# Weights of a two-block transformer: transfers of 8 KB rows, splits of 1024 columns, a gelu of one operation

## The chip, the cores and the metric

One core of a Trainium2 chip runs the whole program in one launch; the batch is one sequence of 256 tokens. The metric is device time in microseconds of one execution, the median of three runs. An engine is written as the profile writes it: PE is TensorE (matmuls; PEld its weight loads), DVE is VectorE, ACT is ScalarE, POOL is GpSimd, SP is the engine whose queue issues nearly all transfers.

## The reference

Two blocks, all in float32, D = 1024, 256 tokens.

- First block, one layer. An rmsnorm and one wide projection `w_in` give a gated linear recurrence (conv of 4 taps, sigmoid gates, a scan), a differential attention of 4 heads and a forgetting attention of 8 heads. Three gated branches are merged and projected. Then `u = causal_dwconv(h @ ffn_up)` with 2816 gate and 2816 value columns, and `x + (gelu(u_gate) * u_val) @ ffn_down`, where gelu is the tanh form.
- Second block, two layers. A mixer (a dilated attention of 12 small heads and a window attention of 16 heads, gates, two branches, an output projection), then 16 experts of width 1024 with expert-choice routing: `softmax(h @ w_router)`, each expert takes its 32 best tokens, and
  `a = xe @ w_gate; u = xe @ w_up; ye = (silu(a) * u) @ w_down` is added back, weighted by the router.

The weights are read once: 141 MB (of 2^20 bytes) of dense weights and 192 MB of expert weights in each of the two layers.

## The kernel before

**Layout.** Activations lie with features on the 128 partitions and the 256 tokens along the free axis; x is `[128, 8, 256]`. Dense weights are packed on the host into loads of 1 MB, `[128, 2048]`: 16 blocks of 128x128.

**Dense work.** `load` (L115) brings one such MB in two transfers of 512 KB (128 rows of 4 KB) into two tiles of a ring of six (`R1 = 6`, `RW = 1024` columns). For float32 accuracy each weight is used as a rounded high part and a low part. `split_w` (L123) makes them for half a load (1024 columns) in two steps of 512 columns: ScalarE copies the high part into `wh` (L129), and VectorE and GpSimd in turn subtract it from the weight, for the low part `wl` (L132):

```python
nc.scalar.copy(wh, s)
turn[0] += 1
eng = nc.gpsimd if turn[0] % 2 == 0 else nc.vector
eng.tensor_tensor(wl, s, wh.bitcast(F32), op=ALU.subtract)
```

The pool of splits has eight `wh` and eight `wl` of 2 KB in a partition, so four halves of a load. The activations are split too (`h[0]` is Ha, `h[1]` is Hb), and `mm3` (L138) issues three matmuls for a block: high by high, high by low, low by high (L139 to L141). A load is therefore 48 matmuls of 256 columns.

**First block.** Stages in order: q, k, v of the two attentions with the attentions between them, the recurrence and its gates, the branch products, the output projection, 22 tiles of the up-projection, and the down-projection. A tile of the up-projection (L627) is one load, `over_rms` (L222) from PSUM, a conv of three taps for the gate and the value part (one ScalarE operation at L252 and two VectorE operations at L256 each), `gelu2` (L243: a square and a tanh on ScalarE, two VectorE operations at L246 and L248), the product with the value part (L639) and `split_act` (L166, L167). Its high parts go to Ah, its low parts to Ala (16 tiles) and Alb (6 tiles, the last ones).

**Mixers.** 23 loads of `w_in2`, 5 of `w_br2` and 4 of `w_out2`, with the window attention and the dilated attention between them. The window attention leaves one of its two softmax scalings to GpSimd (L845).

**Experts.** For each of four groups of four experts, gate, up and down are streamed through. `grouped` (L1208) multiplies the tokens of four experts, 32 partitions of PSUM each, by their weights, k after k; a matmul (L1219) has 32 stationary columns and 512 moving ones. Class `Experts` (L1017) decides where each transfer lands. Its list `todo` has (matrix, expert, rows, columns); `load` (L1039) cuts an item into halves of 4 KB in a partition, or gives it a whole place of 8 KB (two row blocks of 4 KB rows). The cycle of places is: 3 halves in the tiles Qb, 15 in pool a (4 of them, `NA0`, exist from the start of the mixer, 11 from the end of its attentions), then the wholes Ha, Hb and two of pool b, then the six tiles of the ring, four halves cut into pieces of 512 columns (2 KB rows) in the pool of splits, and, the first time only, five halves in W and XB. A place is filled again when its last matmul has read it. The last matrix of a layer comes in column pieces (`ENDS` = 512, 256, 256 columns), so that its transfers have rows of 2 KB and then 1 KB.

**Early transfers.** Part of a layer's experts is brought during the mixer. `prefetch` and `pace` issue these loads after chosen dense loads: 7 items after the window attention, then one `pace` after each load of the gates and branches, up to 13 items; two more (Ha, Hb) at the sixth branch tile, and two into pool b after it. A paced load first writes one column of its place from GpSimd, which reads the newest `wl`: the transfer waits for that split.

**Order.** The order within each engine's queue is written down ahead of the run by a list scheduler with its own cost model, from the program's order and the readiness of the operands. Every queue, SP's too, works in order; an instruction that waits holds what stands behind it.

Of the kernel before, what the change touches and what calls it, by code (L numbers as in the profile page):

```python
# [26 lines left out]

def _places(widths):
# [22 lines left out]
R1, RW, NA0, NA, R2B, NSPLIT, SW = 6, 1024, 4, 15, 2, 8, 512  # L51
# [3 lines left out]
PACE = 1  # L55
# [3 lines left out]
def tile_net(ctx: ExitStack, tc: tile.TileContext, a, out):  # L59
# [6 lines left out]
    ring = ctx.enter_context(tc.tile_pool(name="ring", bufs=R1, side="right"))  # L66
# [4 lines left out]
    first = [ring.tile([P, RW], F32, name="w", tag="w") for _ in range(0, CH, RW)]  # L71
    p1 = None

    def start(pool):
# [38 lines left out]
    turn = [0, None]  # L113

    def load(src):  # L115
        ws = []
        for c in range(0, CH, RW):
            w = ring.tile([P, RW], F32, name="w", tag="w")
            nc.sync.dma_start(w, src[:, c : c + RW])
            ws.append(w)  # L120
        return ws

    def split_w(sp, w, hf):  # L123
        his, los = [], []
        for c in range(hf * 1024, hf * 1024 + 1024, SW):
# [7 lines left out]
            turn[1] = wl  # L133
            his.append(wh)
            los.append(wl)
        return his, los
# [148 lines left out]
    def first_block():  # L285
        with ExitStack() as es:
# [31 lines left out]
            dk, dv = [qp.tile([P, 4, T], F32, name=nm, tag="Qb", bufs=3) for nm in ("dk", "dv")]  # L318
# [301 lines left out]
            with tc.tile_pool(name="b1f", bufs=2) as tp:  # L620
# [3 lines left out]
                for n in (4, 2):  # L624
                    Alb = qp.tile([P, n, T], F32R, name="Alb", tag="Qb", bufs=3)
                    Al += [Alb[:, k] for k in range(n)]
                for j in range(DFF_T):  # L627
# [10 lines left out]
                    gelu2(gg, u[:, 0, :])  # L638
# [470 lines left out]
    def experts(l, last, xl, bp, xg, lg, rt):  # L1109
        nonlocal x  # L1110
        with ExitStack() as es:
# [387 lines left out]
```

## Time and profile before

| | |
|---|---|
| median of 3 runs | 1959.91 us (1959.46 to 1960.38) |
| profiled execution | 1959.11 us, span 1957.1 us |
| busy, share of the span | PE 1665.0 us (85%), DVE 848.3 (43%), ACT 676.0 (35%), POOL 431.1 (22%) |
| mean granted TensorE clock | 0.946 of full speed |
| moved | 562.67 MB in 184744 packets, mean 288 GB/s |

The span is the time from the first to the last instruction; the 2.0 us between it and the execution's own time lie around the program. The busy shares are means over stages with different limits: dense stages (0 to about 785 us and 1240 to 1490) and expert stages (the rest), so they are read by stage. A matmul's busy time overlaps that of its neighbours; its pitch is read from counts in a window. MB and GB/s of the profile count 10^6 and 10^9 bytes.

### The profile page before, as it was taken

How to read it: one execution, taken by the hardware profiler on the slowest of the kernel's cores; microseconds unless marked ns; L12 is line 12 of the kernel's file. 1: busy time of each engine (PE TensorE's matmuls, PEld its weight loads, DVE VectorE, ACT ScalarE, POOL GpSimd, SP SyncE). 2: the span in 40 equal slices, each digit the busy share in tenths (PEclk: the TensorE clock that was granted, in tenths of full speed). 3: DMA queues.
4: the chain of work that ended last, by engine and by line, in shares of the span. 5: the costliest groups of instructions: out<-in, count | busy, mean ns of one | idle time of the engine just before them, and what ended most of it. 6: DMA issues, size and time to landing. Idle time of an engine off the chain costs nothing.

```text
span 1957.1 us, 29983 instructions
## 1 busy us (share of the span) xinstructions
PE 1665.0 (85%) x11434; PEld 1142.9 (58%) x11434; DVE 848.3 (43%) x1525; ACT 676.0 (35%) x1436; POOL 431.1 (22%) x368
## 2 busy tenths in 40 slices
PE   8899999998999998777767776999998587867775
PEld 8799999987998898222211211798995121212112
DVE  8578787998488556100000001686582100000001
ACT  5467656666666644000000000576552000000001
POOL 4333354444454253000000000443350000000000
PEclk9899999999999999888998998999999798989988
DMA  6454465444563379899999999854588999999998
GB/s 238 143 184 149 162 200 171 162 156 166 184 234 113 108 286 345 335 408 405 406 406 407 406 409 377 301 182 129 213 293 302 409 406 407 407 407 406 407 403 268
DMA packets 184744, 562.67 MB, mean 288 GB/s; under 512 B 17932, under 2 KB 39320, under 8 KB 184600
## 3 DMA queue, kind: packets, MB, share of 16 engines
q1 hardware_dynamic: 184440, 560.23, 77.1%
q8 instruction: 90, 1.47, 0.3%
q10 hardware_dynamic: 160, 0.52, 0.1%
q14 instruction: 54, 0.44, 0.1%
HBM read 558.84 MB, written 1.85 MB: 286 GB/s over the span
## 4 chain that ended last, share of the span: by engine, by line
PE 54%; DMA 38%; DVE 5%; issue 2%; ACT 1%; SPq 0%; ACTq 0%; DVEq 0%
DMA we<-in_w_expert_up_dram 16%; PE ps_d L139 12%; PE ps_d L141 12%; PE ps_d L140 12%; DMA we<-in_w_expert_down_dram 11%; DMA we<-in_w_expert_gate_dram 10%; PE ps_e L1219 3%; PE ps_g L1219 2%; PE ps_u L1219 2%; PE ps_t L266 1%; PE ps_v L854 1%; DVE wl L132 1%; PE ps_t L1235 1%; DVE u L256 1%; PE ps_s L382 1%
## 5 line engine op out<-in xcount | busy, mean ns | idle before, releaser
L132 POOL TENSOR_TENSOR wl<-w,wh 128x512 fp32r<-128x512 f32 x282 | 396.2, 1410 | 969.4 <-DMA w<-in_w_in_dram 479.2
L141 PE MATMUL ps_d<-Ha,wl 128*128 128x256 f32 x1408 | 405.7, 288 | 6.4 <-DVE wl L132 6.2
L139 PE MATMUL ps_d<-Ha,wh 128*128 128x256 f32 x1408 | 405.0, 288 | 7.0 <-ACT Ha L186 7.0
L140 PE MATMUL ps_d<-Hb,wh 128*128 128x256 f32 x1408 | 403.3, 286 | 2.0 <-DVE Hb L187 1.9
L129 ACT CAST wh<-w 128x512 fp32r<-128x512 f32 x564 | 334.9, 615 | 152.1 <-PE ps_d L140 111.9
L1219 PE MATMUL ps_u<-we,W 128*32 128x512 f32 x984 | 226.3, 731 | 121.2 <-DMA we<-in_w_expert_up_dram 121.2
L132 DVE TENSOR_TENSOR wl<-w,wh 128x512 fp32r<-128x512 f32 x282 | 239.2, 852 | 97.8 <-ACT wh L129 87.2
L141 PEld LDWEIGHTS ps_d<-Ha,wl 128*128 128x128 f32 x1408 | 271.7, 193 | 12.7 <-DVE wl L132 9.1
L139 PEld LDWEIGHTS ps_d<-Ha,wh 128*128 128x128 f32 x1408 | 271.9, 193 | 11.9 <-ACT Ha L186 7.0
L140 PEld LDWEIGHTS ps_d<-Hb,wh 128*128 128x128 f32 x1408 | 271.7, 193 | 5.0 <-DVE Hb L187 2.7
L1219 PE MATMUL ps_e<-we,W 128*32 128x512 f32 (+1 forms) x1152 | 198.2, 599 | 49.9 <-DMA we<-in_w_expert_down_dram 48.6
L1219 PE MATMUL ps_g<-we,W 128*32 128x512 f32 x1024 | 191.7, 656 | 41.9 <-DMA we<-in_w_expert_gate_dram 41.7
L1219 PEld LDWEIGHTS ps_u<-we,W 128*32 128x32 f32 x984 | 51.4, 126 | 279.2 <-DMA we<-in_w_expert_up_dram 172.0
L1219 PEld LDWEIGHTS ps_e<-we,W 128*32 128x32 f32 x1152 | 51.1, 116 | 176.6 <-DMA we<-in_w_expert_down_dram 88.2
L1219 PEld LDWEIGHTS ps_g<-we,W 128*32 128x32 f32 x1024 | 46.9, 116 | 165.8 <-issue 87.1
L1293 ACT ACTIVATE W<-ps_g 128x512 f32<-128x512 f32 x16 | 9.6, 597 | 382.6 <-PE ps_g L1219 369.3
L1295 DVE SCALAR_TENSOR_TENSOR W<-W,ps_u 128x512 f32<-128x512 f32 x16 | 11.0, 688 | 274.2 <-PE ps_u L1219 274.2
L1300 ACT COPY W<-ps_t 128x512 f32<-128x512 f32 x16 | 9.4, 586 | 295.2 <-PE ps_t L1299 295.2
L1249 DVE COPY W<-ps_e 128x512 f32<-128x512 f32 (+1 forms) x18 | 11.4, 632 | 230.3 <-PE ps_e L1219 230.3
L1294 DVE SCALAR_TENSOR_TENSOR W<-W,ps_g 128x512 f32<-128x512 f32 x16 | 11.0, 688 | 201.8 <-ACT W L1293 188.3
L139 PE MATMUL ps_d<-Y,wh 128*128 128x256 f32 x288 | 80.8, 281 | 0.0
L140 PE MATMUL ps_d<-Y,wh 128*128 128x256 f32 x288 | 80.7, 280 | 0.0
(332 smaller groups left out, 2590.4 us busy)
## 6 DMA issues: line engine op xcount, KB each, us to landing
we<-in_w_expert_down_dram SPq DMA_DIRECT2D x178, 512.0 KB, 10.2
we<-in_w_expert_gate_dram SPq DMA_DIRECT2D x176, 512.0 KB, 9.6
we<-in_w_expert_up_dram SPq DMA_DIRECT2D x156, 512.0 KB, 10.2
w<-in_w_in_dram SPq DMA_DIRECT2D x92, 512.0 KB, 4.4
we<-in_w_expert_up_dram SPq DMA_DIRECT2D x30, 1024.0 KB, 12.7
we<-in_w_expert_gate_dram SPq DMA_DIRECT2D x28, 1024.0 KB, 12.7
w<-in_w_up_dram SPq DMA_DIRECT2D x44, 512.0 KB, 3.7
we<-in_w_expert_down_dram SPq DMA_DIRECT2D x22, 1024.0 KB, 13.1
```

What stands on the lines that cost most here:

```text
L129: nc.scalar.copy(wh, s)
L132: eng.tensor_tensor(wl, s, wh.bitcast(F32), op=ALU.subtract)
L139: nc.tensor.matmul(ps, wh, xh, start=first, stop=False)
L140: nc.tensor.matmul(ps, wh, xl, start=False, stop=False)
L141: nc.tensor.matmul(ps, wl, xh, start=False, stop=last)
L256: nc.vector.scalar_tensor_tensor(dst[:, s:], u[:, : T - s], vec(wname, (taps - 1 - s) * stride + i), dst[:, s:], op0=ALU.mult, op1=ALU.add,)
L266: nc.tensor.transpose(ps[:, i * P : i * P + P], b, ident)
L382: nc.tensor.matmul(pq[c][:, o : o + kr.stop], qs[b, kt, qr], ks[b, kt, kr], start=True, stop=True)
L854: nc.tensor.matmul(po[64 * c : 64 * c + 64, :T], vw[:, k, kvh * 64 : kvh * 64 + 64], pts[c][:, k * T : k * T + T], start=k == 0, stop=k == 1,)
L1219: nc.tensor.matmul(banks[(c0 + c - c_lo) // 512][32 * e : 32 * e + 32, :n], lhs[:, k, 32 * e : 32 * e + 32], cols(ws[e][kk], c, n), start= ...
L1235: nc.tensor.matmul(ps[:, i * P : i * P + P], ht[:, t, k * P : k * P + P], S[:, t].rearrange("p e s -> p (e s)"), start=t == 0, stop=t == 1,)
L1249: nc.vector.tensor_copy(ye[:, s], E[:, :cn])
```

## The change

- Ring and splits: `load` fetches a dense load in one transfer of 128 rows of 8 KB into one of three tiles of 8 KB. `split_w` splits half a load, 1024 columns, with one ScalarE copy and one VectorE subtract into a tile `ws` that holds both parts; four such tiles. GpSimd makes no low parts.
- Experts: the host packs them into 192 chunks of `[128, 2048]` per layer, four experts by 512 columns of one k (in the column pieces of 256, two k). A chunk is one transfer of 128 rows of 8 KB into one place of 8 KB. `grouped` takes one chunk for each k and each PSUM bank. Only the last chunk of a layer goes in two transfers.
- Places: 1 in Qb, 4 in pool a from the start of the mixer, 6 from the end of its attentions, Ha, Hb, 1 in pool b, 3 in the ring, 4 in the pool of splits, and the first time 2 in W and XB.
- Early transfers: one after each of four window-query loads, one after the first load of the dilated attention, then one `pace` per load up to 11; two at the sixth branch tile and one into pool b stay or follow. The paced write from GpSimd stays.
- The up-projection's gelu is one ScalarE operation, and the product with the value part a plain multiply. The recurrence's gelu stays as it was.
- `kl` moves from Qb into the mixer's attention pool; dk and dv share one tile Qb, and Alb is one tile. The scratch reserved for GpSimd's own transfers is set to 2048 bytes.

```diff
-R1, RW, NA0, NA, R2B, NSPLIT, SW = 6, 1024, 4, 15, 2, 8, 512
+RING, NA0, NA, NB, NSPLIT = 3, 4, 6, 1, 4
...
     def load(src):
-        ws = []
-        for c in range(0, CH, RW):
-            w = ring.tile([P, RW], F32, name="w", tag="w")
-            nc.sync.dma_start(w, src[:, c : c + RW])
-            ws.append(w)
-        return ws
+        w = ring.tile([P, CH], F32, name="w", tag="w")
+        nc.sync.dma_start(w, src)
+        return w
 
     def split_w(sp, w, hf):
-        his, los = [], []
-        for c in range(hf * 1024, hf * 1024 + 1024, SW):
-            wh = sp.tile([P, SW], F32R, name="wh", tag="wh")
-            wl = sp.tile([P, SW], F32R, name="wl", tag="wl")
-            s = cols(w, c, SW)
-            nc.scalar.copy(wh, s)
-            turn[0] += 1
-            eng = nc.gpsimd if turn[0] % 2 == 0 else nc.vector
-            eng.tensor_tensor(wl, s, wh.bitcast(F32), op=ALU.subtract)
...
+        ws = sp.tile([P, 2, 1024], F32R, name="ws", tag="ws")
+        s = w[:, hf * 1024 : hf * 1024 + 1024]
+        nc.scalar.copy(ws[:, 0], s)
+        nc.vector.tensor_tensor(ws[:, 1], s, ws[:, 0].bitcast(F32), op=ALU.subtract)
+        turn[0] = ws[:, 1]
+        return ws[:, 0], ws[:, 1]
...
                     gg = tp.tile([P, T], F32, name="fg", tag="fg")
-                    gelu2(gg, u[:, 0, :])
-                    nc.vector.scalar_tensor_tensor(gg, gg, 0.5, u[:, 1, :], op0=ALU.mult, op1=ALU.mult)
+                    nc.scalar.activation(gg, u[:, 0, :], AF.Gelu_apprx_tanh)
+                    nc.vector.tensor_tensor(gg, gg, u[:, 1, :], op=ALU.mult)
...
             for i in range(4):
                 parts_q(qws[i], load(w1[l, 2 + i]))
+                xl.prefetch(1, True)
...
-            xl.prefetch(3 + NA0, True)
...
             parts_q(qa0, load(w1[l, 6]))
+            xl.prefetch(1, True)
...
+            self.cycle = ["q"] + ["a0"] * NA0 + ["a1"] * NA + ["Ha", "Hb"] + ["b"] * NB + ["r"] * RING + ["s"] * NSPLIT
+            self.places = self.cycle + ["x", "x"]
...
+                t = pool.tile([P, CH], F32, name="we", tag=tag)
+            if paced:
+
+                nc.gpsimd.tensor_copy(t[:, 0:1], turn[0][:, 0:1].bitcast(F32))
+            src = a["w_exp"][self.l, i]
+
+            for c0, cn in ((0, 1024), (1024, 1024)) if i == NCHUNK - 1 else ((0, CH),):
+                with tc.issue_after(self.dma.ins) if end else nullcontext():
+                    self.dma = nc.sync.dma_start(t[:, c0 : c0 + cn], src[:, c0 : c0 + cn])
...
+        def pace(self):
+
+            if len(self.have) < 1 + NA0 + NA:
                 self.load(True)
...
-            xl.extra = [W[:, 0], W[:, 1], W[:, 2], XB[:, 0], XB[:, 1]]
+            xl.extra = [W[:, 0:2], XB]
...
+            def grouped(lhs, banks, cn=512, ahead=None):
+
+                kn = 512 // cn
+                for k0 in range(0, KT, kn):
+                    for b in banks:
+                        w = xl.take()
                         if ahead:
-                            ahead(k0 + kk + 1)
...
+                            ahead(k0 + 1)
+                        for k in range(k0, k0 + kn):
                             for e in range(4):
                                 nc.tensor.matmul(
...
+                                    b[32 * e : 32 * e + 32, :cn], lhs[:, k, 32 * e : 32 * e + 32],
+                                    cols(w, ((k - k0) * 4 + e) * cn, cn), start=k == 0, stop=k == KT - 1,
                                 )
```

## Rows read from the trace of the kernel before

**Rows 1.** The page, 40 slices of the span: GB/s.

```profile
...
GB/s 238 143 184 149 162 200 171 162 156 166 184 234 113 108 286 345 335 408 405 406 406 407 406 409 377 301 182 129 213 293 302 409 406 407 407 407 406 407 403 268
...
```

**Rows 2.** Windows: busy us (xcount) PE PEld DVE ACT POOL, PEclk, DMA, GB/s.

```profile
...
782.00:790.00 8.00, 6.87 (x34) 3.21 (x37) 1.40 (x5) 0.53 (x2) 0.00 (x0) 0.52 0.04 17
790.00:1236.00 446.00, 328.62 (x1794) 101.95 (x1786) 34.40 (x60) 21.16 (x48) 0.00 (x0) 0.91 1.03 401
...
1498.00:1943.00 445.00, 326.89 (x1752) 95.05 (x1749) 32.41 (x53) 20.67 (x47) 0.00 (x0) 0.90 1.03 401
...
```

**Rows 3.** Windows of 50 us in the first block, the same columns.

```profile
...
400.00:450.00 50.00, 46.11 (x363) 44.22 (x363) 49.93 (x83) 31.45 (x67) 21.66 (x16) 1.00 0.49 161
450.00:500.00 50.00, 42.04 (x322) 40.55 (x322) 39.05 (x65) 32.06 (x65) 22.88 (x17) 0.93 0.50 167
500.00:550.00 50.00, 50.00 (x420) 50.00 (x420) 27.78 (x52) 34.59 (x65) 21.70 (x18) 1.00 0.58 193
...
```

**Rows 4.** Waits, 0 to 780: waiter, awaited, us in total, times, longest.

```profile
...
ACT wh L129 <- PE ps_d L140: 85.5, 109, 3.0
...
PE ps_d L141 <- DVE wl L132: 7.0, 14, 0.8
...
```

**Rows 5.** Timeline of VectorE, one tile: start, us, instruction.

```profile
...
415.87 0.68 DVE L132 TENSOR_TENSOR wl<-w,wh 128x512 fp32r<-128x512 f32 x1
...
417.40 1.16 DVE L639 SCALAR_TENSOR_TENSOR fg<-fg,u 128x256 f32<-128x256 f32 x1
...
420.27 1.51 DVE L256 SCALAR_TENSOR_TENSOR u<-up,p,u 128x254 f32<-128x254 f32 x1
...
422.37 0.68 DVE L132 TENSOR_TENSOR wl<-w,wh 128x512 fp32r<-128x512 f32 x1
...
```

**Rows 6.** Timeline of GpSimd, the same stretch.

```profile
...
416.99 1.29 POOL L132 TENSOR_TENSOR wl<-w,wh 128x512 fp32r<-128x512 f32 x1 [2.00 <-ACT wh L129]
420.03 1.46 POOL L132 TENSOR_TENSOR wl<-w,wh 128x512 fp32r<-128x512 f32 x1 [1.75 <-ACT wh L129]
...
```

**Rows 7.** Lines 639 and 256: duration ns min/median/max, first and last start.

```profile
...
L639 DVE SCALAR_TENSOR_TENSOR fg<-fg,u x22: 411/1147/1524, 340.5 to 476.7; 128x256 f32<-128x256 f32 x22
...
L256 DVE SCALAR_TENSOR_TENSOR u<-up,p,u x88: 468/476/1558, 332.3 to 473.6; 128x255 f32<-128x255 f32 x44, 128x254 f32<-128x254 f32 x44
...
```

**Rows 8.** DMA counts of 1000:1100, 1190:1200, 1212:1225 and 544:552 us.

```profile
...
DMA packets 12165, 40.67 MB, mean 407 GB/s; under 512 B 1222, under 2 KB 1222, under 8 KB 12161
...
DMA packets 1993, 3.87 MB, mean 387 GB/s; under 512 B 129, under 2 KB 129, under 8 KB 1993
...
DMA packets 4566, 4.53 MB, mean 348 GB/s; under 512 B 144, under 2 KB 4566, under 8 KB 4566
...
DMA packets 432, 1.84 MB, mean 229 GB/s; under 512 B 48, under 2 KB 48, under 8 KB 432
...
```

**Rows 9.** Timeline of the SP queue around the first idle gap.

```profile
...
775.88 1.08 SPq L1055 DMA_DIRECT2D XB<-in_w_expert_up_dram  x2
789.49 1.75 SPq L1055 DMA_DIRECT2D we<-in_w_expert_up_dram  x4
...
```

**Rows 10.** The page's groups: ScalarE's copy of a split.

```profile
...
L129 ACT CAST wh<-w 128x512 fp32r<-128x512 f32 x564 | 334.9, 615 | 152.1 <-PE ps_d L140 111.9
...
```

**Rows 11.** Lines 167 and 166, forms of 1024 columns: ns min/median/max.

```profile
...
L167 DVE TENSOR_TENSOR Y<-vv,Y x2: 1216/1220/1225, 182.5 to 244.7; 128x1024 fp32r<-128x1024 f32 x2
...
L167 DVE TENSOR_TENSOR Y<-od,Y x1: 2322/2322/2322, 169.1 to 169.1; 128x1024 fp32r<-128x1024 f32 x1
...
L166 ACT CAST Y<-vv x2: 1047/1048/1050, 181.4 to 243.6; 128x1024 fp32r<-128x1024 f32 x2
...
```

**Rows 12.** Timeline of TensorE, end of the up-projection.

```profile
...
475.48 0.58 PE L140 MATMUL ps_d<-Alb,wh 128*128 128x256 f32 x1 [2.51 <-DVE Alb L167]
...
```

**Rows 13.** Line 247, tanh inside gelu: ns min/median/max.

```profile
...
L247 ACT ACTIVATE fg<-fg x22: 416/418/421, 339.3 to 475.8; 128x256 f32<-128x256 f32 x22
...
L247 ACT ACT_TABLE_LOAD  x1: 1283/1283/1283, 338.0 to 338.0; - x1
...
```

More of the change, by code (lines that the diff above doesn't have):

```diff
@@ L26 @@
 DFF_T = 22
+NCHUNK = 192
 def _places(widths):
@@ L70, in tile_net @@
     cv = cp.tile([P, NCV], F32, name="cv")
-    first = [ring.tile([P, RW], F32, name="w", tag="w") for _ in range(0, CH, RW)]
+    first = ring.tile([P, CH], F32, name="w", tag="w")
     p1 = None
@@ L623, in first_block @@
                 Al = [Ala[:, k] for k in range(16)]
-                for n in (4, 2):
-                    Alb = qp.tile([P, n, T], F32R, name="Alb", tag="Qb", bufs=3)
-                    Al += [Alb[:, k] for k in range(n)]
+                Alb = qp.tile([P, DFF_T - 16, T], F32R, name="Alb", tag="Qb")
+                Al += [Alb[:, k] for k in range(DFF_T - 16)]
                 for j in range(DFF_T):
@@ new lines, in __init__ @@
+            self.l, self.r2a, self.r2b, self.at, self.dma = l, [], None, 0, None
+            self.have, self.n = [], 0
+            self.cycle = ["q"] + ["a0"] * NA0 + ["a1"] * NA + ["Ha", "Hb"] + ["b"] * NB + ["r"] * RING + ["s"] * NSPLIT
+            self.places = self.cycle + ["x", "x"]
+        def load(self, paced=False):
+            i = len(self.have)
+            end = i >= NCHUNK - sum(cn for _, cn in ENDS) * KT // 512
+            while True:
+                where = self.places.pop(0)
+                if not self.places:
+                    self.places = list(self.cycle)
+                if not (end and where in ("Ha", "Hb")):
+                    break
+            if where == "x":
+                t = self.extra.pop(0).rearrange("p a d -> p (a d)")
+            elif where == "s":
+                t = sp.tile([P, 2, 1024], F32, name="we", tag="ws").rearrange("p a d -> p (a d)")
+            else:
+                pool, tag = {
+                    "q": (qp, "Qb"), "a0": (self.r2a[0], "w2"), "a1": (self.r2a[-1], "w2"), "b": (self.r2b, "w3"),
+                    "r": (ring, "w"), "Ha": (hp, "Ha"), "Hb": (hp, "Hb"),
+                }[where]
+                t = pool.tile([P, CH], F32, name="we", tag=tag)
[5 more added lines that the diff above has]
+                    self.dma = nc.sync.dma_start(t[:, c0 : c0 + cn], src[:, c0 : c0 + cn])
+            self.have.append(t)
@@ L1281, in experts @@
                     S = slots(g, pt_)
+                seen = []
                 gather(0)
@@ L1358, in _flat, with _experts @@
     return b.transpose(0, 2, 1, 3).reshape(-1, P, CH)
+def _experts(*ws):
+    chunks = []
+    for g in range(4):
+        for w in ws:
+            w = w[4 * g : 4 * g + 4]
+            if len(chunks) == 11:
+                for c0, cn in ENDS:
+                    b = w[:, :, c0 : c0 + cn].reshape(4, cn * KT // 512, 512 // cn, P, cn)
+                    chunks.append(b.transpose(1, 3, 2, 0, 4).reshape(-1, P, CH))
+            else:
+                chunks.append(w.reshape(4, KT, P, 2, 512).transpose(1, 3, 2, 0, 4).reshape(-1, P, CH))
+    return np.concatenate(chunks, 0)
 def _cols(v):
```

127 lines of the change are left out of this document (24 added, 103 removed).

## The prediction

> **What bounds the kernel now.** I read the slices of the page first, then windows of 50 us, then the timeline of one repeating tile, then the DMA packets of single stretches, and the issues of the queue last. The GB/s line [rows 1] shows two kinds of stage: dense stages with 100 to 250 GB/s, and two long plateaus at 405 to 409, which are the expert layers. In the plateaus TensorE waits for weights: from 790 to 1236 us and from 1498 to 1943 us it is busy 328.6 of 446 and 326.9 of 445 us, while the DMA share is 1.03 [rows 2]. These 891 us are as long as their bytes divided by the rate. In the dense stages it is the other way round. A dense stretch without stalls has 420 matmuls in 50 us [rows 3], a pitch of 0.119 us; a load (1 MB of weights, 48 matmuls) costs 5.73 us and needs 183 GB/s. Splits run ahead there: ScalarE's copies waited 85.5 us for TensorE to free a place, and TensorE waited only 7.0 us in 14 pieces for a subtract [rows 4].
>
> One dense stage is an exception: the up-projection of the first block (about 328 to 475 us). VectorE is busy 49.93 of 50 us, TensorE gets through 363 matmuls where 420 fit, and in the next window through 322 [rows 3]. The same subtract comes again after 6.50 us (415.87 to 422.37) [rows 5], against the 5.73 us that 48 matmuls need. Two VectorE operations in each tile are stretched, one of 256 columns to 1.16 us and one of 254 to 1.51 us [rows 5]; both start inside a GpSimd subtract (416.99 to 418.28, 420.03 to 421.49) [rows 6]. Their unstretched times are 0.411 and 0.468 us [rows 7].
>
> **The change, part by part.** Durations come from the one profiled execution: 1959.1 us with a span of 1957.1, 0.8 us under the median 1959.9.
>
> *Row size of the expert weights.* Per packet of one of the 16 engines, from the DMA counts [rows 8]: 1 KB rows (1212 to 1225 us) moved 4.53 MB at 348 GB/s, so 1024 / (348/16) = 47.1 ns; 2 KB rows (1190 to 1200) 387 GB/s, so 84.7 ns. The difference is 37.6 ns per KB, and 9.5 ns are left for each packet. Checked at 4 KB: 9.5 + 150.4 = 159.9 ns or 410 GB/s; the stretch 1000 to 1100, 4 KB rows with some of 2 KB, has 407. An 8 KB row would take 9.5 + 300.8 = 310.3 ns, so 422 GB/s; with the same 0.8% shortfall, 419. No row of 8 KB is in this trace. The bounds are 407 (an 8 KB row goes as two packets, no gain) and 16 x 1024 / 37.6 = 435 (no cost per packet). The nearest row is the only longer one: between 544 and 552 us one load with 6 KB rows and two of 4 KB moved 1.84 MB in 432 - 48 = 384 data packets [rows 8]. That is 128 + 256, so a 6 KB row is one packet. I take 419. The last 16 MB of each layer, now in rows of 2 KB and 1 KB, are in 8 KB rows too, so the plateau's mean of 401 [rows 2] rises more than its best stretch does.
>
> The Trainium skill has a smaller price, in "DMA: Bandwidth & Descriptors", "Why small descriptors are slow (HBM only)": about 3 bus cycles per packet beside one cycle per 32 bytes. By it 4 KB rows gain 1.2% (an estimate from the page: 2 x 131 / 259), 407 becomes 412, and my sum below would end at 1903 us. The trace disagrees: by the page 1 KB rows would reach 94% of the rate of 4 KB rows; [rows 8] have 348 / 407 = 86%.
>
> *Bytes that are left when the plateau starts.* Before it runs, the places that need no expert to be finished hold 3 + 15 halves, Ha, Hb, 2 of pool b, 6 ring halves, 4 split halves and 5 extra halves: 20.5 MB (of 2^20). After: 1 + 4 + 6 + 2 + 1 + 3 + 4 + 2 = 23. The queue had nothing to issue between 776.9 and 789.5 us [rows 9] and moved only 17 GB/s from 782 to 790 [rows 2], since all places were full and the router's chain held TensorE up. Eight idle us at 407 GB/s hold 3.3 MB, so 2.6 MB more fit into them. A plateau moves 445 x 401 = 178.4 MB; 175.8 remain. At 419 GB/s that is 419.6 us: 25.4 us less per layer, **50.8 us for two**. At 407 it is 431.9 (13.1 per layer), at 435 it is 404.1 (40.9). If the 2.6 MB do not fit, 6.3 us per layer come back.
>
> *Splits without GpSimd.* Per load ScalarE has four copies of 0.615 us [rows 10], 2.46; then two of 1024 columns at 1.047 [rows 11], 2.09. VectorE has two subtracts of 0.68 (the unstretched ones in [rows 5]); then two of 1.22 [rows 11], so 1.1 us more per load, bounded by 2.32 us each, which is the one stretched case in [rows 11]. In exchange nothing stretches the others. In the up-projection a tile of 6.50 us loses 1.16 - 0.41 + 1.51 - 0.47 = 1.79, loses two of the three gelu operations at 0.41 (0.82), and gains 1.1: 5.0 us, under the 5.73 of TensorE. TensorE is the bound again; 0.77 us come back per tile where the backlog exists. Counted in matmuls that are missing: 57 in 400 to 450 and 98 in 450 to 500 us, 155 x 0.119 = 18.4 us [rows 3]. This includes the tail, where TensorE stood until 475.48 for the last tile's low part [rows 12], at the end of the same backlog; a smaller backlog before 400 is not counted. I take **19 us**, bounds 10 and 23. If VectorE stays at over 5.73 us per tile, the stage is late by the difference times 22.
>
> *Gelu in one operation.* Two VectorE operations and one of ScalarE less, counted above. The one operation is priced as the tanh it replaces, 0.418 us [rows 13]. ScalarE is busy 31.45 of 50 us in that stage [rows 3], 4.1 us per tile; less 0.37 of the copies and one operation of 0.42 it has 3.3, hidden by TensorE's 5.73 even if the new operation took five times as long.
>
> *The other dense stages.* TensorE has no stall to give back while its count stands at 420 in 50 us [rows 3], so the GpSimd relief is worth nothing there. At a stage's first split TensorE waits for 1.05 + 1.22 instead of 0.62 + 0.69 us, 1.0 us more; this comes in some four places (start, two mixers, the first tile after an attention). The chains of small VectorE operations between dense work, stretched by GpSimd now, give about as much back. I take **2 us of gain**, between 8 of loss and 8 of gain, since the written order of the queues shifts with every duration.
>
> *Ring of 3 x 1 MB, pacing, transfers.* Same bytes in flight. A load's first half arrives later by half a megabyte, 1.3 us at 407 GB/s, and the ring holds 3 x 5.73 = 17 us of work, which hides it. A paced expert load waits on GpSimd for the newest split; behind it on the SP queue stand the next dense loads, and TensorE waits for those if the split pool (four halves, 11 us) runs dry. Nothing: the same waits stand in the queue now.
>
> Sum: 50.8 + 19 + 2 = 72 us, 1959.1 - 72 = 1887; with the 0.8 us to the median, **1888 us**.
>
> **Rivals.** (1) *Rows of 8 KB bring no rate*: the engines cut them at 4 KB. The rate stays 407, two layers gain 26, the sum is 47: 1912 us. Against it stands the 6 KB row that was one packet [rows 8]; for it, that nothing longer was seen. (2) *The gap is not filled*: the late places (extra and split) are freed with the last dense work, or the queue puts them behind a wait. Two times 6.3 us back: 1900. For it: the queue's last issues before the gap already come at 776 [rows 9]. (3) *Gelu and the conv's activation are in different tables*: today one load of 1.283 us serves all 22 tiles [rows 13]. Two loads in each tile make ScalarE 3.3 + 2.6 = 5.9 us per tile, 0.2 over TensorE's, and the chain of each tile 2.6 us longer; if half the 19 us go, 1898. The page "ScalarE: Activation LUTs" of the Trainium skill, "Table sets: the hidden batching unit", has the cheap functions such as identity and copy in every set as filler, which speaks against it; no run here shows which sets these are. (4) *Slower: the coarse split falls behind TensorE.* Place: the 282 halves of the dense stages. The first matmul of a half now waits for a whole copy and a whole subtract of 1024 columns, 2.27 instead of 1.31 us. If the pool no longer runs ahead, each half pays up to 0.96 us, 271 us in all; if one in two pays it, 1888 + 135 = 2023. It decides from 0.26 us per half (72 / 282): above that the kernel is slower than before. For it: one VectorE queue now carries all subtracts, 2.44 of 5.73 us. Against: 85.5 us of copies waiting for free places [rows 4], that is, splits a full pool ahead.
>
> **How the numbers follow.** My forecast (some rate gain, the gap filled, the up-projection on TensorE's pace) gets 0.62, rival 1 0.18, rival 2 0.09, rival 3 0.03, rival 4 0.08. The predicted time is the forecast's, 1888. Its own range is 1866 (a rate half way to 435, 33 us per layer, with 23 + 5 of the others) to 1902; rival 1 with the low ends of the other terms (26 + 10 - 8 = 28 us of gain, 1932) is the far end, and most of the way there the range goes: 1925. A difference under 0.2% (4 us) cannot be told from none here. All but rival 4, and a share of bad luck, are faster by much more than that: faster 0.90, within 0.2% 0.03, slower 0.07.
>
> **What would show it.** Right: the plateaus at 417 to 424 GB/s and some 420 us long, with half as many packets; no stretch of 8 us with idle DMA before them; 415 to 420 matmuls per 50 us between 350 and 470; no GpSimd operation beside the paced ones, the mask and the window softmax; no VectorE subtract over 1.3 us outside these. Wrong: the plateaus at 407 (rival 1); table loads at the gelu line (rival 3); TensorE waiting for the subtract in more than a few dozen pieces (rival 4); dense loads landing after ScalarE waits for them.

## The result

The changed kernel takes **1899.07 us** (median of 4 runs, 1896.45 to 1900.42) against 1960.14 for the kernel before on the same chip: ratio 0.9687, 95% interval 0.967 to 0.9704. The forecast was 1888. The profiled execution has 1898.55 us and a span of 1896.8 (before 1957.1), so the account below is of 60.3 us of span.

The profile page of the changed kernel, the busy times, the GB/s line (it answers to [rows 1]) and the packets:

```profile
...
PE 1600.4 (84%) x11434; PEld 1081.8 (57%) x11434; DVE 823.2 (43%) x1481; ACT 629.2 (33%) x1130; POOL 46.3 (2%) x72
...
GB/s 248 167 190 167 178 178 179 187 190 178 217 223 112 147 267 275 397 419 420 420 420 419 420 420 418 332 129 102 222 266 277 418 420 419 419 420 419 420 421 321
DMA packets 83829, 562.49 MB, mean 297 GB/s; under 512 B 9452, under 2 KB 14456, under 8 KB 16888
...
```

The plateaus stand at 419 to 420 GB/s, where [rows 1] have 403 to 409. Windows of the changed kernel, columns as in [rows 2]: both plateaus, the gap ahead of the first, and three stretches of the first block:

```profile
...
758.00:1188.00 430.00, 306.87 (x1820) 73.14 (x1812) 34.37 (x60) 21.27 (x48) 0.00 (x0) 0.77 1.01 416
1456.00:1886.00 430.00, 302.16 (x1792) 67.53 (x1784) 32.32 (x53) 20.75 (x47) 0.00 (x0) 0.78 1.00 414
752.00:760.00 8.00, 5.19 (x22) 2.74 (x26) 2.97 (x8) 0.53 (x2) 0.00 (x0) 0.50 0.02 9
50.00:100.00 50.00, 50.00 (x373) 43.73 (x373) 30.59 (x58) 25.74 (x60) 7.04 (x8) 1.00 0.50 171
350.00:400.00 50.00, 50.00 (x419) 50.00 (x419) 46.39 (x80) 32.52 (x52) 0.00 (x0) 1.00 0.52 183
400.00:450.00 50.00, 50.00 (x420) 50.00 (x419) 42.19 (x71) 32.43 (x52) 0.00 (x0) 1.00 0.53 184
...
```

From 400 to 450 us the up-projection has 420 matmuls, where [rows 3] has 363. The gap of 8 us with an idle DMA ahead of the plateau is still there (9 GB/s from 752 to 760, as 17 in [rows 2]).

Each kernel was then cut at the same landmarks, read from the starts of instructions in its profiled execution. All in us: the first and the last write of VectorE to the tile `up` of the up-projection, the first expert matmul (what lies before it is called the front), the length of plateau 1 (to the last copy of `ps_e`), the middle (from there to the second layer's first expert matmul), plateau 2, and the span.

| kernel | first `up` | last `up` | first expert | plateau 1 | middle | plateau 2 | span |
|---|---|---|---|---|---|---|---|
| before | 330.6 | 469.4 | 785.8 | 451.5 | 255.8 | 452.4 | 1957.1 |
| after | 315.2 | 431.8 | 757.5 | 430.6 | 267.3 | 430.7 | 1896.8 |
| e1_rows4k | 315.9 | 432.4 | 761.1 | 442.0 | 268.0 | 442.8 | 1925.4 |
| e2_gelu4 | 315.9 | 442.1 | 763.5 | 430.6 | 260.5 | 431.1 | 1896.4 |
| e3_poolsub | 329.5 | 448.7 | 771.7 | 429.7 | 266.5 | 430.8 | 1910.0 |
| e4_split512 | 317.2 | 434.6 | 758.7 | 429.8 | 263.8 | 430.6 | 1893.6 |
| e5_before_nopool | 315.7 | 445.0 | 753.0 | 450.2 | 254.3 | 452.0 | 1921.0 |
| e6_ring4 | 314.7 | 431.2 | 753.0 | 433.0 | 258.0 | 434.6 | 1890.0 |
| e8_pace2 | 316.0 | 432.6 | 752.9 | 430.1 | 258.8 | 431.0 | 1883.5 |
| e10_all | 317.0 | 434.4 | 749.4 | 430.2 | 254.4 | 430.6 | 1875.1 |
| e11_pace2_gelu4 | 314.8 | 441.0 | 756.9 | 429.8 | 258.1 | 430.9 | 1886.4 |
| e12_pace2_w0 | 314.8 | 431.4 | 751.8 | 430.9 | 255.4 | 431.0 | 1879.9 |
| e13_pace2_na4 | 315.2 | 431.7 | 752.1 | 434.9 | 259.0 | 436.3 | 1892.9 |
| e14_pace2_rows2k | 315.1 | 431.6 | 751.9 | 480.1 | 258.5 | 484.7 | 1986.9 |

Before to after: the front -28.3, the plateaus -20.9 and -21.7, the **middle +11.5**, the tail -0.9. The tail is what lies behind plateau 2. The puzzle is the middle, which was forecast to stay about as it was and got slower.

Where it lost is seen in TensorE's count in the gate and branch stage of the first mixer (changed kernel; us, PE busy and count, PEclk, DMA share, GB/s). 44 or 45 matmuls in 5 us are full pace:

```profile
...
655.00:660.00 5.00, 5.00 (x44) 1.00 0.98 408
660.00:665.00 5.00, 5.00 (x45) 1.00 1.02 426
665.00:670.00 5.00, 2.80 (x24) 1.00 1.01 421
670.00:675.00 5.00, 4.88 (x41) 1.00 0.96 380
675.00:680.00 5.00, 2.47 (x17) 0.90 0.08 31
680.00:685.00 5.00, 5.00 (x35) 0.76 0.83 290
...
```

About 59 are missing between 665 and 685, 7 us; such a stretch is called a hole below. From 1360 to 1380 the second mixer has 26, 28, 21 and 28, some 8.7 us. Not all of this is waiting: from 680 to 685 TensorE is busy all 5 us and still gets only 35 done, at a granted clock of 0.76, and in the second mixer it twice has 28 at 0.66. Behind the waits of a hole the clock was partly at the lower of its two levels (1.2 instead of 2.4 GHz). The kernel before has no such hole in the same stages (columns as in [rows 2]):

```profile
...
690.00:740.00 50.00, 50.00 (x421) 49.88 (x420) 32.77 (x45) 24.87 (x50) 27.86 (x30) 1.00 0.78 281
1400.00:1450.00 50.00, 50.00 (x423) 50.00 (x422) 34.45 (x45) 24.77 (x49) 27.85 (x23) 1.00 0.83 301
...
```

Three causes were possible: the order of queues (ScalarE's copy stands behind a tanh, VectorE's subtract behind a merge that waits for TensorE), the pieces of 1024 columns, or the DMA, which is full in the ten us before.

### The profile page after: what moved, and what is told of

Read it like the earlier page. It is cut to its first block, busy times and chain, and to the rows that moved or that the text cites. A ratio compares the mean times of both kernels' runs of the same rounds, so it can differ in the third digit from the quotient of the medians.

```text
span 1896.8 us, 27588 instructions
## 1 busy us (share of the span) xinstructions
PE 1600.4 (84%) x11434; PEld 1081.8 (57%) x11434; DVE 823.2 (43%) x1481; ACT 629.2 (33%) x1130; POOL 46.3 (2%) x72
## 4 chain that ended last, share of the span: by engine, by line
PE 54%; DMA 43%; DVE 2%; ACT 1%; issue 0%; SPq 0%; ACTq 0%; DVEq 0%
DMA we<-in_w_exp_dram 42%; PE ps_d L130 14%; PE ps_d L131 14%; PE ps_d L132 14%; PE ps_t L257 1%; PE ps_g L1172 1%; PE ps_v L846 1%; DMA w<-in_w_in_dram 1%; PE ps_u L1172 1%; PE ps_s L772 1%; PE ps_s L878 1%; PE ps_s L773 0%; PE ps_s L374 0%; PE ps_t L1187 0%; PE ps_v L896 0%
## 5 line engine op out<-in xcount | busy, mean ns | idle before, releaser
L130 PE MATMUL ps_d<-Ha,ws 128*128 128x256 f32 x1408 | 404.9, 288 | 14.7 <-ACT Ha L177 7.9
L132 PE MATMUL ps_d<-Ha,ws 128*128 128x256 f32 x1408 | 404.9, 288 | 5.0 <-DVE ws L125 4.9
L131 PE MATMUL ps_d<-Hb,ws 128*128 128x256 f32 x1408 | 403.6, 287 | 0.7 <-DVE Hb L178 0.7
L125 DVE TENSOR_TENSOR ws<-w,ws 128x1024 fp32r<-128x1024 f32 x282 | 342.6, 1221 | 119.7 <-ACT ws L124 117.0
L124 ACT CAST ws<-w 128x1024 fp32r<-128x1024 f32 x282 | 293.3, 1047 | 256.0 <-PE ps_d L132 223.3
L130 PEld LDWEIGHTS ps_d<-Ha,ws 128*128 128x128 f32 x1408 | 273.0, 194 | 18.4 <-ACT Ha L177 7.9
L132 PEld LDWEIGHTS ps_d<-Ha,ws 128*128 128x128 f32 x1408 | 273.0, 194 | 8.3 <-DVE ws L125 6.1
L131 PEld LDWEIGHTS ps_d<-Hb,ws 128*128 128x128 f32 x1408 | 272.9, 194 | 3.5 <-issue 1.2
L1172 PE MATMUL ps_u<-we,W 128*32 128x512 f32 x992 | 187.8, 836 | 90.4 <-DMA we<-in_w_exp_dram 90.3
L1172 PE MATMUL ps_e<-we,W 128*32 128x512 f32 (+1 forms) x1152 | 162.6, 669 | 64.2 <-DMA we<-in_w_exp_dram 64.1
L1172 PEld LDWEIGHTS ps_u<-we,W 128*32 128x32 f32 x992 | 25.4, 125 | 239.2 <-DMA we<-in_w_exp_dram 223.1
L1201 DVE COPY W<-ps_e 128x512 f32<-128x512 f32 (+1 forms) x18 | 11.4, 632 | 221.5 <-PE ps_e L1172 221.5
L130 PE MATMUL ps_d<-Y,ws 128*128 128x256 f32 x288 | 81.4, 283 | 0.0
L132 PE MATMUL ps_d<-Y,ws 128*128 128x256 f32 x288 | 81.4, 283 | 0.0
L131 PE MATMUL ps_d<-Y,ws 128*128 128x256 f32 x288 | 81.4, 282 | 0.0
```

Source lines behind the costliest of these rows:

```text
L124: nc.scalar.copy(ws[:, 0], s)
L125: nc.vector.tensor_tensor(ws[:, 1], s, ws[:, 0].bitcast(F32), op=ALU.subtract)
L130: nc.tensor.matmul(ps, wh, xh, start=first, stop=False)
L131: nc.tensor.matmul(ps, wh, xl, start=False, stop=False)
L132: nc.tensor.matmul(ps, wl, xh, start=False, stop=last)
L1172: nc.tensor.matmul(b[32 * e : 32 * e + 32, :cn], lhs[:, k, 32 * e : 32 * e + 32], cols(w, ((k - k0) * 4 + e) * cn, cn), start=k == 0, stop ...
```

## The experiments

Times are medians of 4 runs; ratios are against the kernel before on the same chip, with 95% intervals. The kernel before itself read 1958.2 to 1960.1 us in these comparisons, so a difference of 2 us between two versions cannot be told from none.

**The rows of 8 KB.** e1_rows4k:

```diff
-for c0, cn in ((0, 1024), (1024, 1024)) if i == NCHUNK - 1 else ((0, CH),):
+for c0, cn in ((0, 1024), (1024, 1024)):
```

> Every expert chunk of 1 MB comes as two DMAs of 512 KB with rows of 4 KB, into the same place; nothing else differs from the changed kernel. Theory A (the length of a row sets the rate): the plateaus fall from 419-420 to 407-410 GB/s; 178 MB at 407 instead of 416-418 is about 10 to 11 us more per layer, so 1899 becomes 1917 to 1921. Rival (the plateaus gained because a chunk is one issue and one place, or because more bytes came early): they stay at 418-420 GB/s and the time within 4 us of 1899.

1926.52 us, ratio 0.9835 (0.982 to 0.9849). The plateaus grew by 11.4 and 12.1 us, a little more than theory A's 10 to 11; another 3.6 came in the front, whose cause isn't shown. The time is 5.5 us above theory A's range. e14_pace2_rows2k (on top of e8_pace2, below) cuts a chunk in four:

```diff
-for c0, cn in ((0, 1024), (1024, 1024)) if i == NCHUNK - 1 else ((0, CH),):
+for c0, cn in ((0, 512), (512, 512), (1024, 512), (1536, 512)):
```

> The version with every second paced chunk (e8_pace2), with every expert chunk as four DMAs of 256 KB with rows of 2 KB. Theory A (each packet costs 9.5 ns beside 36.7 to 37.6 ns per KB, as the rows of the kernel before gave it): 2 KB rows reach about 387 GB/s, 178 MB take 460 us instead of 425, plateaus of 465 us, 1950 to 1958 in all. Rival (only 1 KB rows are dear, and what was slow at the layer's end before was its order): 400 GB/s or more, under 1925. By the page 'DMA: Bandwidth & Descriptors' of the Trainium skill, 'Why small descriptors are slow (HBM only)', 2 KB rows would be 3.4% slower than 8 KB rows, an estimate of 405 GB/s and about 1914.

1989.78 us, ratio 1.0154 (1.0139 to 1.017), slower even than the kernel before, and 32 us above theory A's range: the plateaus are 480 and 485 us, not 465. DMA counts from 900 to 1000 us, e1_rows4k and then e14_pace2_rows2k:

```profile
...
DMA packets 11219, 40.90 MB, mean 409 GB/s; under 512 B 1246, under 2 KB 1246, under 8 KB 11215
...
```

```profile
...
DMA packets 20727, 37.79 MB, mean 378 GB/s; under 512 B 2302, under 2 KB 2302, under 8 KB 20723
...
```

The mean rates of 2, 4 and 8 KB rows are 378, 409 and 420 GB/s (the last from 900 to 1000 us of the changed kernel): for one of 16 engines 86.7, 160.2 and 312.1 ns per packet. The steps are 36.8 and 38.0 ns per KB, which leaves 13 and 8 ns for each packet; the prediction's 9.5 lies between. Most slices of 2.5 us of the 2 KB run show 379 to 397 GB/s, around the 387 of [rows 8]; five slices of 306 to 345 pull the mean down, and what made them isn't shown. In these kernels rows and DMAs shrink together (1 MB, 512 KB, 256 KB), as they do in the kernel before. The engines did not stand idle for want of issues: their busy share in the three stretches is 101.1, 102.4 and 103.8% with rows of 8, 4 and 2 KB. Whether a smaller DMA has a price of its own beside that of its rows was not separated. The estimate of 405 for 2 KB rows, from the page "DMA: Bandwidth & Descriptors" of the Trainium skill that the expectation names, is refuted by the 378.

**GpSimd.** e5_before_nopool changes the kernel before in one line:

```diff
-            eng = nc.gpsimd if turn[0] % 2 == 0 else nc.vector
+            eng = nc.vector
```

> The kernel before with all subtracts of the weight splits on VectorE (512 columns each); nothing else changed. Theory A (GpSimd's two-input work held the dense front back): the up-projection goes to TensorE's pace (near 420 matmuls in 50 us) and the stall of the first 60 us goes; the first expert matmul comes 15 to 25 us before 785.8, and the time is 1935 to 1945, since the plateaus stay at 451 us. Rival (the front was gained by gelu in one operation and by the larger places): the first expert matmul moves by less than 5 us and the time stays above 1953.

1922.90 us, ratio 0.9819 (0.9805 to 0.9834): more gain than theory A's bound. Plateaus and middle stay within 1.5 us; the front gets 32.8 us shorter: 14.9 until the first `up` tile, 9.5 in the up-projection, 8.4 behind it. e3_poolsub goes the other way, the changed kernel with GpSimd back:

```diff
+        turn[1] += 1
-        nc.vector.tensor_tensor(ws[:, 1], s, ...
+        (nc.gpsimd if turn[1] % 2 == 0 else nc.vector).tensor_tensor(ws[:, 1], s, ...
```

> The changed kernel with every second subtract of a split (1024 columns) on GpSimd. Theory A (two-input work on GpSimd stretches VectorE's): the up-projection is bound by VectorE again, operations of 0.41 us take over 1 us, the first expert matmul comes 10 to 25 us later than 757.6; in the gate and branch stages of the mixers the second queue lets a subtract pass the merge that waits for TensorE, so the holes there shrink; in all 1905 to 1920. Rival (the gain of the dense stages came from gelu and from the larger places): the first expert matmul stays within 4 us of 757.6 and the time is 1885 to 1899, lower by the holes in the mixers.

1910.12 us, ratio 0.9747 (0.9731 to 0.9764). The time is theory A's, the way to it only in part. The first `up` tile comes 14.3 us later, the first expert matmul 14.2. VectorE's operations beside GpSimd are stretched again (tile `fg`, ns min/median/max, e3_poolsub and then the changed kernel):

```profile
...
L159 DVE TENSOR_TENSOR Ala<-fg,Ah x16: 419/2038/2191, 340.5 to 420.5; 128x256 fp32r<-128x256 f32 x16
...
```

```profile
...
L158 DVE TENSOR_TENSOR Ala<-fg,Ah x16: 413/418/422, 325.2 to 405.2; 128x256 fp32r<-128x256 f32 x16
...
```

The up-projection, however, kept TensorE's pace, against my theory (windows of e3_poolsub, columns as in [rows 2]):

```profile
...
350.00:400.00 50.00, 50.00 (x419) 50.00 (x418) 50.00 (x72) 34.46 (x54) 23.12 (x9) 1.00 0.52 189
400.00:450.00 50.00, 50.00 (x419) 50.00 (x418) 50.00 (x72) 34.50 (x53) 20.48 (x9) 1.00 0.53 190
...
```

What GpSimd costs before 330 us is shown only as a sum. From 50 to 100 us the kernel before has 278 matmuls, e5_before_nopool 361 and the changed kernel 373; from 150 to 200 us they have 375, 408 and 408. In GpSimd's queue of the kernel before a subtract stands behind the mask's operation, which waits 8.25 us for a DMA:

```profile
...
55.08 1.23 POOL L419 TENSOR_TENSOR cm<-cm,p 128x256 f32<-128x256 f32 x2 [8.25 <-DMA cm<-nck_d]
56.27 1.26 POOL L132 TENSOR_TENSOR wl<-w,wh 128x512 fp32r<-128x512 f32 x1
...
```

No wait of TensorE ended there, though. Its one long wait in that stretch was 7.50 us, until 61.56, for VectorE's `z`, and this `z` stood in VectorE's queue behind an operation that waited 9.24 us for the load of `lq` (kernel before: TensorE's waits from 40 to 110 us in total, times and longest, then VectorE's timeline):

```profile
...
PE ps_s L382 <- DVE z L422: 7.5, 1, 7.5
...
```

```profile
...
58.17 0.46 DVE L448 TENSOR_TENSOR lt<-lq 128x64 f32<-128x64 f32 x1 [9.24 <-DMA lq<-in_rows_dram]
...
60.97 0.54 DVE L422 SCALAR_TENSOR_TENSOR z<-ps_s,cm 128x384 f32<-128x384 f32 x1
...
```

In e5_before_nopool the written order has the first `z` ahead of that operation (59.38 and 61.39), and TensorE waits 1.19 us. The clock adds to the loss: behind the wait of 7.50 us it was granted at 0.52 from 60 to 70 us, where e5_before_nopool has 1.00. Taking the subtracts from GpSimd thus also changed the written order of other queues; how much of the 14.9 us each of the two is worth was not separated. In e3_poolsub the loss lies more in the other stretch: 345 matmuls from 50 to 100, 350 from 150 to 200.

**Gelu.** e2_gelu4 and e11_pace2_gelu4 (the same on e8_pace2):

```diff
-nc.scalar.activation(gg, u[:, 0, :], AF.Gelu_apprx_tanh)
-nc.vector.tensor_tensor(gg, gg, u[:, 1, :], op=ALU.mult)
+gelu2(gg, u[:, 0, :])
+nc.vector.scalar_tensor_tensor(gg, gg, 0.5, u[:, 1, :], op0=ALU.mult, op1=ALU.mult)
```

> The changed kernel with gelu in the four operations of the kernel before (two on ScalarE, two on VectorE, and the scaled product). Theory A (GpSimd's leaving alone put the up-projection back on TensorE's pace): VectorE's queue gets 0.82 us more per tile, 42-46 busy of 50 us become 49-53, TensorE's count falls by a few per 50 us, the time rises by 0 to 3 us. Rival (gelu carries a good part of the gain of the up-projection): the stage is VectorE-bound again, some 0.3 to 0.6 us per tile, 7 to 13 us more, 1906 to 1912.

1898.56 us, ratio 0.9692 (0.9677 to 0.9706), no difference from the changed kernel. But the last `up` tile came 10.3 us later, the first expert matmul 6.0, and the middle, where no gelu is, was 6.8 shorter: the hole there was smaller in this kernel (why, below), and that hid the loss. So the question was put again without the holes:

> The version with every second paced chunk (e8_pace2), with gelu in the four operations of the kernel before; here no hole of the gate stage can hide or feign a difference. Theory A (one operation instead of four is worth something, since the four bring VectorE's queue to some 5.8 us per tile against TensorE's 5.73): the last up-projection tile comes 8 to 10 us later, as in e2_gelu4, the first expert matmul 3 to 8 us later than 752.9, and the time is 1888 to 1892. Rival (the front's gain is GpSimd's alone, and a late last tile is caught up by the splits that run ahead): within 1.5 us of 1884.5.

1888.20 us, ratio 0.9639 (0.9623 to 0.9655), 3.7 above e8_pace2; last `up` tile 8.4 later, first expert matmul 4.0. The one operation is worth some 4 us. It is one table load for 22 tiles (ScalarE's groups in the changed kernel), so rival 3 is out:

```profile
...
L629 ACT ACTIVATE fg<-u 128x256 f32<-128x256 f32 x22 | 9.1, 416 | 0.0
...
L629 ACT ACT_TABLE_LOAD x1 | 1.3, 1283 | 0.0
...
```

**The holes.** e4_split512 (on the changed kernel):

```diff
-        nc.scalar.copy(ws[:, 0], s)
-        nc.vector.tensor_tensor(ws[:, 1], s, ws[:, 0].bitcast(F32), op=ALU.subtract)
+        for c in (slice(0, 512), slice(512, 1024)):
+            nc.scalar.copy(ws[:, 0, c], s[:, c])
+            nc.vector.tensor_tensor(ws[:, 1, c], s[:, c], ws[:, 0, c].bitcast(F32), op=ALU.subtract)
```

> The changed kernel with each half split in two pieces of 512 columns (copy, subtract, copy, subtract), all on VectorE, in the same places. Theory A (the pieces of 1024 columns make the holes of the gate and branch stages): TensorE's count in 665 to 685 us goes back to about 44 per 5 us, 5 to 8 us come back in each mixer and 1 to 2 at each start of a stage: 1883 to 1890. Rival (the holes come from the order of one queue: the subtract stands behind merge operations that wait for TensorE, the copy behind a tanh that does): they stay, and the time is 1897 to 1903, with 0.28 us more per load on VectorE.

1897.01 us, ratio 0.9685 (0.967 to 0.9699): the holes stayed (16 and 6 matmuls from 670 to 680 us). Coarse pieces aren't their cause. Neither is one VectorE queue alone: in e3_poolsub half of the subtracts had another queue, and the middle was 266.5. Nor the size of an expert transfer: e1_rows4k brings the same chunks as two transfers of 512 KB, and its middle is 268.0. That left the DMA and the order of ScalarE's queue. e6_ring4 has one dense load more ahead, e8_pace2 fewer expert chunks between:

```diff
-RING, NA0, NA, NB, NSPLIT = 3, 4, 6, 1, 4
+RING, NA0, NA, NB, NSPLIT = 4, 3, 6, 1, 4
```

> The changed kernel with a ring of four dense loads instead of three, and one early place less in the first pool (3 instead of 4), so that as many expert chunks fit. Theory A (the holes of the gate and branch stages come from a dense load that lands late behind a burst of expert chunks): a fourth load ahead covers most of it, the holes shrink from 7 and 8.6 us to 2 or less each, 1884 to 1890. Rival (the order of the queues makes them: a copy behind a tanh, a subtract behind a merge): they stay, 1897 to 1902.

```diff
         def pace(self):
+            self.at += 1
-            if len(self.have) < 1 + NA0 + NA:
+            if self.at % 2 == 0 and len(self.have) < 1 + NA0 + NA:
```

> The changed kernel with one paced expert chunk after every second dense load of the gate and branch stages instead of every one, so the six chunks are spread over twelve loads. Theory A (burst of expert chunks): the DMA share stays under 0.9 in the 15 us behind the closing of the attention, TensorE's count in the holes goes back to about 44 per 5 us, 12 to 16 us are gained in the two mixers: 1883 to 1889; the plateaus keep their length if all 23 early chunks still land before they begin. Rival (the order of the queues): the holes stay where they were, 1896 to 1902.

e6_ring4: 1891.98 us, ratio 0.9657 (0.9643 to 0.9672). e8_pace2: **1884.47 us**, ratio 0.9618 (0.9602 to 0.9634). In both the holes are gone. e8_pace2 in the same stretch:

```profile
...
660.00:665.00 5.00, 5.00 (x44) 1.00 1.01 378
665.00:670.00 5.00, 5.00 (x44) 1.00 0.54 184
670.00:675.00 5.00, 5.00 (x44) 1.00 0.29 120
675.00:680.00 5.00, 5.00 (x44) 1.00 0.97 364
...
```

e6_ring4 keeps the burst (418 to 428 GB/s from 655 to 675) and still has 44, so a full DMA does no harm by itself when one more dense load is ahead. Its plateaus are 2.4 and 3.9 us longer: 22 chunks came early there, not 23 as I had expected. Issues from 655 to 661 us in the changed kernel (count, KB, median us to landing):

```profile
...
we<-in_w_exp_dram SPq DMA_DIRECT2D x3, 1024.0 KB, 12.6
w<-in_w_in_dram SPq DMA_DIRECT2D x2, 1024.0 KB, 13.4
...
```

The 13.4 us are those of one dense load, issued at 658.48 among the chunks; the landing of the other is not in the trace. A dense load issued to an idle DMA takes 4.7 (e8_pace2, at 650.96).

The late load is only one part of the cause. It landed at 671.9, but ScalarE copied it only at 676.45: in the written order the copy stands behind a tanh whose input TensorE had still to make. e2_gelu4 shows that this order matters. Its mixers have the same code and its load is as late (issued at 666.89, 13.5 us to landing), but there the written order has the copy ahead of the tanh, and ScalarE takes the load as it lands. ScalarE, the changed kernel and then e2_gelu4:

```profile
...
675.64 0.91 ACT L927 ACTIVATE tg<-tg,hb 128x256 f32<-128x256 f32 x2 [7.27 <-DVE tg L213]
676.45 2.93 ACT L124 CAST ws<-w 128x1024 fp32r<-128x1024 f32 x3
...
```

```profile
...
680.45 2.19 ACT L124 CAST ws<-w 128x1024 fp32r<-128x1024 f32 x2 [3.66 <-DMA w<-in_w_in_dram]
684.83 1.05 ACT L124 CAST ws<-w 128x1024 fp32r<-128x1024 f32 x1 [2.19 <-PE ps_d L132]
685.78 0.90 ACT L927 ACTIVATE tg<-tg,hb 128x256 f32<-128x256 f32 x2
...
```

Its holes are smaller: 37 matmuls are missing where the changed kernel misses 59, and 25 where it misses 73 in the second mixer. In e8_pace2 and e6_ring4 the written order differs too: eight and nine copies stand between the end of the attention and this tanh, nine in e2_gelu4, six in the changed kernel. So each of the two edits changed the loads and, with them, the order. That either edit takes the holes away is shown; how much of that is the order is not.

**The change of the layer.** In the changed kernel the next layer's first load lands behind the last chunks. ScalarE and then TensorE there, changed kernel:

```profile
...
1190.11 1.99 ACT L124 CAST ws<-w 128x1024 fp32r<-128x1024 f32 x2 [7.95 <-PE ps_g L1207]
...
1192.46 0.58 PE L132 MATMUL ps_d<-Ha,ws 128*128 128x256 f32 x1 [0.46 <-DVE ws L125]
...
```

The load was issued at 1174.67 and took 15.0 us to land. The last copy of `ps_e` was at 1188.08, so 4.4 us pass until TensorE's first matmul with a low part (L132); in the kernel before the same distance is 1.7 us (1237.29 to 1238.97). e12_pace2_w0 loads it in halves:

```diff
-w0 = load(a["w_in2"][l + 1, 0])
+w0 = ring.tile([P, CH], F32, name="w", tag="w")
+for c in range(0, CH, 1024):
+    nc.sync.dma_start(w0[:, c : c + 1024], a["w_in2"][l + 1, 0, :, c : c + 1024])
```

> The version with every second paced chunk (e8_pace2), with the first load behind an expert layer as two DMAs of 512 KB into its place; the splits stay at 1024 columns. Theory A (TensorE waits there for the whole megabyte): its first half lands 1.25 us earlier, the stretch from the last E copy to the first expert matmul of the second layer falls from 258.8 by 1 to 3 us, time 1881.5 to 1883.5. Rival (what is waited for is the whole copy and the whole subtract of 1024 columns, so that the 512-column pieces of e10_all brought its 6 us): within 1 us of 1884.5.

1880.84 us, ratio 0.96 (0.9586 to 0.9614), 3.6 below e8_pace2, a little more than theory A's 1 to 3; the middle fell by 3.4. e10_all has this, the pacing and the pieces of 512 columns:

> The changed kernel with three edits: paced chunks after every second dense load, the splits in pieces of 512 columns, and the first load behind an expert layer in two DMAs of 512 KB. If the holes come from the burst and the wait at the layer's change from the whole megabyte and its whole split: 12 to 16 us from the mixers, 3 to 5 from the change of the layer: 1878 to 1886. If the holes come from the queues' order: 1892 to 1898, the change of the layer alone.

**1878.55 us** (1876.92 to 1880.71), ratio 0.959 (0.9576 to 0.9604), the best version: 20.5 us below the changed kernel. Against e12_pace2_w0 the pieces of 512 columns are worth 2.3 us, which is not clear of noise: the two intervals overlap.

**Early places.** e13_pace2_na4 has NA = 4 instead of 6 on e8_pace2:

> The version with every second paced chunk (e8_pace2), with 4 late places instead of 6 in the second early pool, so two chunks (2.1 MB) per layer fewer come before the plateau. Theory A (the plateau is what is left of the bytes over a fixed rate): 2.1 MB / 419 GB/s = 5.0 us more per layer, plateaus of 435 us, 1894.5 in all, and the idle stretch of the DMA before the plateau grows by as much as the bytes took there. Rival (the early places are worth less, since they crowd the dense loads, or a place more in the plateau's own cycle is what counts): less than 4 us in all.

1894.93 us, ratio 0.9671 (0.9657 to 0.9685): plateaus 4.8 and 5.3 us longer, 10.5 us in all. A byte that comes early is worth what it would take on the plateau.

## Why the prediction came out as it did

The forecast of 1888 us was 11 short of 1899. That it came so near is in part luck: terms that were too high by some 35 us stand against terms that were too low by some 23.

**Row size: right.** 419 GB/s was forecast, 419 to 420 measured; rival 1 is out. e1_rows4k gives 11.4 and 12.1 of a plateau's 20.9 and 21.7 us to 8 KB against 4 KB. The rest, some 9.5 per layer, lies between e1_rows4k and the kernel before, whose last 16 MB per layer had rows of 2 and 1 KB. By the GB/s of the plateau's last five slices of 11.3 us (399, 386, 350, 348 and 363, against some 409 in e1_rows4k) these rows make an estimated 5.5 of the 9.5.

**Bytes that are left when the plateau starts: the term that was mis-sized.** The forecast took off 2.6 MB per layer, 6.3 us. DMA counts of the first plateau, kernel before (786 to 1237) and changed kernel (758 to 1188):

```profile
...
DMA packets 60918, 179.18 MB, mean 397 GB/s; under 512 B 5449, under 2 KB 13641, under 8 KB 60899
...
```

```profile
...
DMA packets 24845, 179.05 MB, mean 416 GB/s; under 512 B 2878, under 2 KB 2878, under 8 KB 3134
...
```

The bytes are the same; the gain is the mean rate alone: 179.18 MB / 397 = 451 us, 179.05 / 416 = 430. The prediction had counted places in the code. The issues of the kernel before, 470 to 786 us, say otherwise:

```profile
...
we<-in_w_expert_gate_dram SPq DMA_DIRECT2D x24, 512.0 KB, 6.9
...
we<-in_w_expert_gate_dram SPq DMA_DIRECT2D x4, 1024.0 KB, 7.7
we<-in_w_expert_up_dram SPq DMA_DIRECT2D x8, 256.0 KB, 4.8
we<-in_w_expert_down_dram SPq DMA_DIRECT2D x8, 256.0 KB, 4.8
W<-in_w_expert_up_dram SPq DMA_DIRECT2D x3, 512.0 KB, 6.4
XB<-in_w_expert_up_dram SPq DMA_DIRECT2D x2, 512.0 KB, 6.8
...
```

That is 12 + 4 + 2 + 2 + 1.5 + 1 = 22.5 MB (of 2^20), not 20.5: the split pool gave 16 places of 256 KB, not 8. The changed kernel's 23 (21 `we`, `W`, `XB`) are 0.5 more. The two plateaus were forecast to gain 50.8 us and gained 42.6; of the forecast, 12.6 (two times 6.3) were for bytes that came early in the kernel before already. This has the size of rival 2 and not its reason: no late place was missed, all were full ahead of the gap in both kernels.

**The up-projection: right in size.** The forecast was 19 us; from its first to its last tile the stage fell from 138.8 to 116.6, 22.2. Without GpSimd's subtracts alone it fell by 9.5 (e5_before_nopool), and the stretched operations of [rows 7] were back at 418/422/449 ns (L639). Put back into the changed kernel, GpSimd costs the stage 2.6 us (e3_poolsub), the four operations of gelu 9.6 (e2_gelu4): with both reliefs VectorE is busy 42 to 46 of 50 us, and TensorE is the bound, as the prediction had it.

**"The other dense stages": wrong, both ways.** "The GpSimd relief is worth nothing there" went by one window of 420 matmuls behind 500 us [rows 3]; before the first `up` tile, where the stretch from 50 to 100 us had only 278, came 15.4 us; e5_before_nopool alone gains 14.9 there. The coarse pieces, priced at 1.0 us in some four places, cost some 2 us at most (e10_all against e12_pace2_w0, within the noise).

**"Ring of 3 x 1 MB, pacing, transfers ... Nothing": wrong.** The forecast priced half a megabyte more at 1.3 us and took 17 us of work in the ring to hide it. It named the paced chunks ahead of dense loads on the queue, and put them at nothing. A dense load among chunks took 13.4 us to land, ScalarE's order added 4.5 before it was copied, and the holes cost 13.1 (4.6 before the first expert matmul and 8.5 in the middle, changed kernel against e8_pace2). The whole megabyte at the change of the layer costs 3.4 more.

Against the forecast of 72 us, then: plateaus -8.2 (12.6 of bytes too much, 4.4 of rate too little), holes -13.1, change of the layer -3.4; before the first `up` tile +15.4, up-projection +3.2. The other -6 are the 2 us put down for the other stages and 4 that e8_pace2, which has no holes, loses between the last `up` tile and the first expert matmul (320.3 against 316.4). The coarse split did not fall behind by itself: ScalarE's copies still waited 223.3 us for TensorE to free places, and rival 4 is out.

Rival 1 was also priced too low: with 4 KB rows and everything else changed the kernel takes 1926.5 us (e1_rows4k), not 1912.

Three things are open: what the late load and the written order are worth each in the holes, what made the 14.9 us before the first `up` tile, and the last 4 us behind the up-projection.

## What to carry to other kernels

Where a stage moves bytes at the full rate, price a row by its packets, and count early bytes by the issues in the trace, not by the places in the code. Where urgent and early loads share a queue, look at when the urgent ones land: spreading the early ones took 14.6 us off the median here, one urgent load more ahead 7.1. Then look at what stands ahead of the landed load in the next engine's queue. Where the order of the queues is written by a scheduler, an edit in one stage can change it in another, so compare the order itself before a difference is put down to the edit; and a part whose effect is nil should be tried again once other stalls are out, as gelu shows.

## What the runs showed of the hardware

Not expected: TensorE's mean granted clock on the first plateau is 0.91 of full speed in the kernel before [rows 2] and 0.77 in the changed one, and the mean over the whole execution is 0.982 in e1_rows4k against 0.888 in the changed kernel. No cost of it shows on the plateau: the changed kernel, with the lowest clock of the three, has the shortest plateau, TensorE is busy 306.87 of its 430 us, and the DMA share is 1.01.
